# Operand tiles of the MLP's up weights at 24 offsets inside larger buffers

## The chip, the cores and the metric

The kernel runs on one core of a Trainium2 chip. The metric is device time in microseconds (us). Engines: TensorE (PE, its weight load PEld), VectorE (DVE), ScalarE (ACT), GpSimd (POOL) and SyncE (SP), whose queue issues the DMA transfers here.

## The reference

One layer with 1024 tokens of width 1024, in float32: an RMS norm, one input projection, two groups of heads in parallel (differential attention and a gated delta rule), an output projection added to the input, and then a squared-ReLU MLP of hidden width 4096. The change lies in the MLP's first half:

```python
h = rms_norm(x, norm2_w[l])
x = x + jnp.square(jax.nn.relu(h @ w_up[l])) @ w_down[l]
```

## The kernel before

Float32 products are made from a high and a low half: a tensor is cast to `fp32r` (the high half, on ScalarE), the cast is subtracted from the original (the low half, on VectorE), and TensorE multiplies high by high, low by high and high by low, three matmuls for one. `split` does the two steps.

The up stage multiplies `w_up` by the normed tokens. It saves products by Strassen's scheme (in Winograd's form): per group `g` of 512 hidden columns (8 groups) the weights come as four raw tiles a, b, c, d of 128 x 1024 elements, the tokens as four blocks and their differences (`hH`, `hL` and `T0h` to `T2l`), and seven products, numbered 1 to 7, take the place of eight. A product is 24 matmuls of 512 columns (2 column halves x 4 blocks x 3). "Product (0,6)" below is product 6 of group 0.

Products 3, 5, 6 and 7 need a sum or difference of raw tiles, made on VectorE (`combine`, L1443). The weights of a product then become an operand, a pair of tiles named `op`: the cast (L1447 in `rounded`, L1243 in `split`) and the subtraction (L1451 in `rest`, L1244 in `split`). The pool has five `op` buffers of 128 x 1024 elements, used in turn; they are TensorE's stationary operand, the tokens its moving one (`prod_up`, L1324 to L1326). After a product ScalarE or VectorE reads its PSUM bank (X, Y or Z) and forms the results `ua`, `b`, `c`, `ud`, `s`, which SP stores to DRAM for the down stage (`flush`, L1437). SP also loads the raw tiles (L1416), each when its buffer is free.

The first products of group 0 and 1 use operands made earlier, in the weight buffers of the stages before (`first_ops`: `wH0`, `wH1`, `wL0`): products (0,1), (0,2), (1,1), (1,2), in that order, into X0, Y, X1 and Z. X1's stationary operand in its first product lies in `wH1`. Then come (0,5), (0,6), (0,3), (0,7), (1,5), (0,4), (1,6), and so on. The operands of (0,5), (0,6), (0,3) and (0,7) are made by `rounded` and `rest`, in an order written out by hand.

A buffer may take memory that an earlier stage has given up; its first writer then waits for that tile's last reader. The five `op` buffers lie at the top of the memory that the weight buffers leave. In the built program the first `op` buffer begins at byte 208704 of a partition, where the raw buffers `wraw` were (208128 to 212287), and the last ends at 229184. `wH1` was at 199488 to 207807, `wL0` at 212288 to 220607. Below the `op` buffers lie `s`, `c`, `ud` and `b`.

Up to the marker `seam.close()` the order of TensorE, VectorE and ScalarE is the order of the code; behind it TensorE alone keeps the code's order, and a scheduler places VectorE's and ScalarE's instructions by its own model of their times.

The last stage multiplies the results by `w_down` (`down`, L1619 to L1621).

Of the kernel before, what the change touches and what calls it, by code (L numbers as in the profile page):

```python
# [10 lines left out]
F32R = mybir.dt.float32r  # L11
# [7 lines left out]
P = 128  # L19
# [98 lines left out]
def tile_hymba_layer(  # L118
# [491 lines left out]
    for h, hf, y, th in skew(dn_proj(1)):  # L610
# [6 lines left out]
        for c in range(4):  # L617
            i = cidx(h, 4 * hf + c)
# [9 lines left out]
        for c in range(4):  # L628
            i = cidx(h, 4 * hf + c)
# [49 lines left out]
    for h, hf, q2 in skew(dn_proj(0)):  # L679
# [6 lines left out]
        for c in range(4):  # L686
            i = cidx(h, 4 * hf + c)
# [3 lines left out]
        for c in range(4):  # L691
            i = cidx(h, 4 * hf + c)
# [548 lines left out]
    def split(dst, src):  # L1241

        S.copy(dst[0], src)  # L1243
        V.tensor_tensor(dst[1], src, dst[0].bitcast(F32), ALU.subtract)  # L1244
# [147 lines left out]
    op_ = octx.enter_context(tc.tile_pool(name="op", bufs=1, **right))  # L1392
# [16 lines left out]
    def load_w(g, names):  # L1409
        if g < NG:  # L1410
            u.setdefault(g, {})
            for n in names:
# [3 lines left out]
                nc.sync.dma_start(t, w_up_v[:, (k1, k2)[i % 2], c:c + 256])  # L1416
                w.setdefault(g, {})[n] = t

    def operand(src):
        o = [op_.tile([P, 4, 256], F32R, tag="op", name="op", bufs=5) for _ in range(2)]  # L1420
        split(o, src)
        return o

# [15 lines left out]
    early = {}  # L1439
# [3 lines left out]
        V.tensor_tensor(w[g][dst], w[g][l], w[g][r], op)  # L1443

    def rounded(g, i):
        early[g, i] = [op_.tile([P, 4, 256], F32R, tag="op", name="op", bufs=5) for _ in range(2)]
        S.copy(early[g, i][0], w[g][CH[i]])  # L1447

    def rest(g, i):
# [9 lines left out]
    held(2, [0, 1])  # L1459
    combine(0, 5)  # L1460
    rounded(0, 5)
    held(0, [2, 3])
    held(1, [2])
    rest(0, 5)
    held(1, [3])
    read_first()
    combine(0, 6)
    rounded(0, 6)
    combine(0, 3)
    held(2, [2, 3])  # L1470
# [4 lines left out]
    def product(g, i):  # L1475
# [10 lines left out]
        else:  # L1486
            bank = [x[:, p] for p in range(2)]
        o = early.pop((g, i), None) or (operand(w[g][CH[i]]) if g > 1 or i > 2 else None)
        for p in range(2) if o else ():
            for _ in prod_up(bank[p], o, p, H_OPS[i], i in (1, 2, 5) or (i == 4 and last), i in (2, 3, 4)):  # L1490
# [45 lines left out]
    def step(g, i):  # L1536
        puts.append([])
        product(g, i)
        flush(2)

    rounded(0, 3)
    step(0, 5)
    rest(0, 3)
# [154 lines left out]
```

## Time and profile before

| what | value |
|---|---|
| median of 3 runs | 1269.35 us (1268.46 to 1269.78) |
| profiled execution: span from first to last instruction | 1272.0 us; the page gives no other time of that execution |
| TensorE busy | 1238.8 us, 97% of the span |
| VectorE, ScalarE, GpSimd busy | 842.6, 602.7, 212.3 us |
| up stage, first and last matmul on `op` tiles | starts 673.61 us and 956.47 us |
| down stage | from 958.53 us to the end |

The rows below are of three kinds. A row of the timeline has the start in us, the duration in us, the engine, the line, the operation, its output and inputs, its shape and count, and in brackets the idle time of the engine before it with what ended it. A row of a tile or line has the durations in ns (least/median/most) and the first and last start. A row of a stretch has, for each engine, the busy us and the instructions, then the granted clock, the DMA engines' share and GB/s. Buffer numbers are left out of names: X is X0 or X1.

### The profile page before, as it was taken

What the parts mean: (1) busy time and instruction counts of PE and PEld (TensorE: products, weight loads), DVE (VectorE), ACT (ScalarE), POOL (GpSimd) and SP (SyncE); (2) the same over time, 40 slices, a digit from 0 to 9 for tenths busy, and PEclk for the clock granted to TensorE, in tenths of its full rate; (3) what the DMA queues carried; (4) which work ended last, traced back from release to release, by engine and by line L of the source; (5) the groups of instructions that cost most, each with busy time, mean ns of one, the idle gap of its engine ahead of it and who ended that gap; (6) DMA issues with size and microseconds to landing.
All of it is one profiled execution on the core that took longest, in us unless ns stands there. A gap on an engine that the chain in (4) does not pass through costs nothing.

```text
span 1272.0 us, 18929 instructions
## 1 busy us (share of the span) xinstructions
PE 1238.8 (97%) x6928; PEld 1066.1 (84%) x6928; DVE 842.6 (66%) x1406; ACT 602.7 (47%) x1176; POOL 212.3 (17%) x240
## 2 busy tenths in 40 slices
PE   8999999999999899999999999999999999999998
PEld 7977888898998898888878888888887788888886
DVE  5569798467727775776689656655667865677553
ACT  5354554334445565655467445445554333333331
POOL 1038222135543542122210000000000000000000
PEclk9999999999998999999999999999999999999999
DMA  7134554367674665333354545443368855422311
GB/s 251 50 108 110 152 163 126 82 189 236 214 212 143 191 191 168 100 107 92 130 172 160 204 149 182 160 154 116 132 211 323 325 198 199 165 100 100 125 41 66
DMA packets 164757, 200.29 MB, mean 157 GB/s; under 512 B 20224, under 2 KB 124984, under 8 KB 164664
## 3 DMA queue, kind: packets, MB, share of 16 engines
q1 hardware_dynamic: 164664, 199.08, 47.4%
q8 instruction: 55, 0.90, 0.3%
q14 instruction: 38, 0.31, 0.1%
HBM read 132.97 MB, written 66.06 MB: 156 GB/s over the span
## 4 chain that ended last, share of the span: by engine, by line
PE 86%; DVE 7%; DMA 3%; issue 2%; ACT 1%; POOL 1%; SPq 1%; DVEq 0%; POOLq 0%; ACTq 0%
PE X L1326 5%; PE X L1324 5%; PE X L1325 5%; PE X L1620 4%; PE X L1621 4%; PE X L1619 4%; PE ps_qk L909 3%; PE ps_qk L910 3%; PE ps_qk L911 3%; PE Y L1326 2%; PE Y L1324 2%; PE Y L1325 2%; PE ps_dn L202 2%; PE ps_o L1070 2%; PE ps_dn L204 2%; PE ps_dn L203 2%
## 5 line engine op out<-in xcount | busy, mean ns | idle before, releaser
L1243 ACT CAST hH<-ur 128x1024 fp32r<-128x1024 f32 x56 | 58.7, 1050 | 176.5 <-PE Z L1620 86.0
L1244 DVE TENSOR_TENSOR hL<-ur,hH 128x1024 fp32r<-128x1024 f32 x56 | 68.4, 1223 | 84.8 <-ACT hH L1243 84.7
L909 PE MATMUL ps_qk<-wH,hH 128*128 128x256 f32 x384 | 115.3, 300 | 0.0
L910 PE MATMUL ps_qk<-wL,hH 128*128 128x256 f32 x384 | 109.8, 286 | 0.0
L911 PE MATMUL ps_qk<-wH,hL 128*128 128x256 f32 x384 | 109.7, 286 | 0.0
L1244 DVE TENSOR_TENSOR op<-raw,op 128x1024 fp32r<-128x1024 f32 x48 | 58.7, 1223 | 74.1 <-PE X L1325 36.9
L1620 PE MATMUL X<-hL,hH 128*128 128x512 f32 x224 | 87.8, 392 | 2.1 <-DVE hL L1244 2.1
L1619 PE MATMUL X<-hH 128*128 128x512 f32 x224 | 87.5, 391 | 1.7 <-DVE b L1521 1.7
L1621 PE MATMUL X<-hH,hL 128*128 128x512 f32 x224 | 87.6, 391 | 0.0
L202 PE MATMUL ps_dn<-hH,wH 128*128 128x512 f32 x192 | 76.8, 400 | 1.7 <-ACT cp L525 1.7
L203 PE MATMUL ps_dn<-hL,wH 128*128 128x512 f32 x192 | 76.3, 397 | 0.0
L204 PE MATMUL ps_dn<-hH,wL 128*128 128x512 f32 x192 | 75.9, 396 | 0.0
L910 PEld LDWEIGHTS ps_qk<-wL,hH 128*128 128x128 f32 x384 | 74.6, 194 | 0.2
L909 PEld LDWEIGHTS ps_qk<-wH,hH 128*128 128x128 f32 x384 | 74.7, 195 | 0.0
L911 PEld LDWEIGHTS ps_qk<-wH,hL 128*128 128x128 f32 x384 | 74.4, 194 | 0.0
L1244 DVE TENSOR_TENSOR hL<-dw,hH 128x1024 fp32r<-128x1024 f32 x56 | 68.1, 1218 | 4.8 <-ACT hH L1243 4.8
L1243 ACT CAST op<-raw 128x1024 fp32r<-128x1024 f32 x48 | 50.4, 1051 | 35.7 <-PE Y L1326 19.9
L1243 ACT CAST hH<-dw 128x1024 fp32r<-128x1024 f32 x56 | 58.4, 1047 | 13.8 <-PE Z L1621 7.4
L197 POOL TENSOR_TENSOR wL<-wraw,wH 128x512 fp32r<-128x512 f32 x40 | 51.9, 1311 | 69.9 <-ACT wH L196 47.5
L529 DVE SCALAR_TENSOR_TENSOR cy<-cp,pv,cy 128x512 f32<-128x512 f32 x72 | 57.6, 804 | 7.9 <-ACT cy L527 7.2
L1031 ACT ACTIVATE pexp<-ps_sc,mx 128x128 f32<-128x128 f32 (+7 forms) x64 | 47.3, 741 | 25.9 <-DVE mx L1027 25.4
L1027 DVE TENSOR_REDUCE mx<-ps_sc 128x1 f32<-128x128 f32 (+7 forms) x64 | 47.6, 753 | 16.1 <-PE ps_sc L1025 15.5
(360 smaller groups left out, 3527.4 us busy)
## 6 DMA issues: line engine op xcount, KB each, us to landing
ur<-ud SPq DMA_DIRECT2D x28, 1024.0 KB, 4.9
raw<-in_w_up_dram SPq DMA_DIRECT2D x32, 512.0 KB, 3.9
dw<-in_w_down_dram SPq DMA_DIRECT2D x32, 512.0 KB, 6.5
wraw<-in_w_in_dram SPq DMA_DIRECT2D x48, 256.0 KB, 3.2
qk_d<-qa SPq DMA_DIRECT2D x32, 256.0 KB, 2.9
ud<-ua SPq DMA_DIRECT2D x16, 512.0 KB, 3.0
ud<-s SPq DMA_DIRECT2D x16, 512.0 KB, 2.6
pka<-park_d SPq DMA_DIRECT2D x32, 192.0 KB, 3.6
```

The lines of the kernel that those rows point to most:

```text
L202: T.matmul(ps, lh(k), rh(k), start=(k == 0), stop=False)
L203: T.matmul(ps, lh(k), rl(k), start=False, stop=False)
L204: T.matmul(ps, ll(k), rh(k), start=False, stop=(k == n - 1))
L909: T.matmul(ps[:, :256], hH[:, k, sl], wh[:, k, :], start=(k == 0), stop=False)
L910: T.matmul(ps[:, :256], hH[:, k, sl], wl[:, k, :], start=False, stop=False)
L911: T.matmul(ps[:, :256], hL[:, k, sl], wh[:, k, :], start=False, stop=(k == KB - 1))
L1243: S.copy(dst[0], src)
L1244: V.tensor_tensor(dst[1], src, dst[0].bitcast(F32), ALU.subtract)
L1324: T.matmul(ps, op[0][:, k, cs], h[0][:, k, :], start=start and k == 0, stop=False, skip_group_check=True)
L1619: T.matmul(bank[t], v[0][:, j, sl], v[2][:, j], start=s0, stop=False, skip_group_check=True)
L1620: T.matmul(bank[t], v[0][:, j, sl], v[3][:, j], start=False, stop=False, skip_group_check=True)
L1621: T.matmul(bank[t], v[1][:, j, sl], v[2][:, j], start=False, stop=s1, skip_group_check=True)
```

## The change

Each `op` tile becomes 128 x 1088 elements, and the 1024 elements in use begin at an offset that goes by turn: the first tile of pair n at entry n of a list of 24 offsets, the second at entry 7n + 3, both modulo 24. The offsets run from 0 to 60 elements of 4 bytes. Both places that make operands, `operand` and `rounded`, get their pairs from the new function.

```diff
+    SHIFTS = (0, 1, 2, 3, 4, 5, 6, 7, 8, 10, 12, 14, 16, 18, 20, 24, 28, 32, 36, 40, 44, 48, 52, 60)
+    made = [0]
+
+    def op_pair():
+        n, k = made[0], len(SHIFTS)
+        made[0] += 1
+        return [op_.tile([P, 1088], F32R, tag="op", name="op", bufs=5)[:, s:s + 1024].rearrange("p (k c) -> p k c", k=4)
+                for s in (SHIFTS[n % k], SHIFTS[(7 * n + 3) % k])]
+
     def operand(src):
-        o = [op_.tile([P, 4, 256], F32R, tag="op", name="op", bufs=5) for _ in range(2)]
+        o = op_pair()
         split(o, src)
         return o
...
     def rounded(g, i):
-        early[g, i] = [op_.tile([P, 4, 256], F32R, tag="op", name="op", bufs=5) for _ in range(2)]
+        early[g, i] = op_pair()
         S.copy(early[g, i][0], w[g][CH[i]])
```

No instruction is added or taken away. In the built program the `op` buffers now begin at 207424, 211776, 216128, 220480 and 224832; `s`, `c`, `ud` and `b` lie 1280 bytes lower, and 207424 lies inside what was `wH1`. The first cast into `op` (L1447 before, L1456 now) accordingly waits for the last matmul into X1 that reads `wH1`, where it had waited for the last matmul into Y that reads `wL0`; both also wait for the combined raw tile. TensorE's order is unchanged. Lines from L1419 on are 9 higher than before.

On VectorE some rows behind the operand of (0,7) change places. The engine's rows before, from the low half of operand (0,7) on; the next two operands are those of (1,5) and (0,4):

```order
L1451 TENSOR_TENSOR op<-raw,op 128x1024
L1244 TENSOR_TENSOR T2l<-kept,T2h 128x4x128 x2
L1443 TENSOR_TENSOR raw<-raw 128x1024
L1244 TENSOR_TENSOR T2l<-kept,T2h 128x4x128 x2
L1497 TENSOR_TENSOR ua_8488<-ua_8488,Z_8309 128x512
L1497 TENSOR_TENSOR ua_8488<-ua_8488,Z_8310 128x512
L1505 TENSOR_TENSOR c<-c,Y 128x1024
L1244 TENSOR_TENSOR op<-raw,op 128x1024 x2
L1510 TENSOR_TENSOR ud<-ud,X_7845 128x1024
L1443 TENSOR_TENSOR raw<-raw 128x1024
L1507 TENSOR_TENSOR s_8521<-ua_8383,c 128x1024
L1443 TENSOR_TENSOR raw<-raw 128x1024 x2
```

The same stretch of the change:

```order
L1460 TENSOR_TENSOR op<-raw,op 128x1024
L1452 TENSOR_TENSOR raw<-raw 128x1024
L1244 TENSOR_TENSOR T2l<-kept,T2h 128x4x128 x4
L1506 TENSOR_TENSOR ua_8488<-ua_8488,Z_8309 128x512
L1506 TENSOR_TENSOR ua_8488<-ua_8488,Z_8310 128x512
L1244 TENSOR_TENSOR op<-raw,op 128x1024
L1514 TENSOR_TENSOR c<-c,Y 128x1024
L1452 TENSOR_TENSOR raw<-raw 128x1024 x2
L1244 TENSOR_TENSOR op<-raw,op 128x1024
L1519 TENSOR_TENSOR ud<-ud,X_7845 128x1024
L1516 TENSOR_TENSOR s_8521<-ua_8383,c 128x1024
L1452 TENSOR_TENSOR raw<-raw 128x1024
```

The combination for (1,5) now stands ahead of the four rows of `T2l`, the operand of (1,5) ahead of `c<-c,Y`, and two combinations ahead of the operand of (0,4). On ScalarE one cast moves; before:

```order
L1370 ACTIVATE c<-c 128x1024
L1371 ACTIVATE c<-c 128x1024
L1370 ACTIVATE ud<-ud 128x1024
L1371 ACTIVATE ud<-ud 128x1024
L1243 CAST op<-raw 128x1024
L1501 COPY ud<-Y 128x1024
```

and of the change:

```order
L1370 ACTIVATE c<-c 128x1024
L1371 ACTIVATE c<-c 128x1024
L1243 CAST op<-raw 128x1024
L1370 ACTIVATE ud<-ud 128x1024
L1371 ACTIVATE ud<-ud 128x1024
L1510 COPY ud<-Y 128x1024
```

The cast of the operand of (1,6) goes ahead of the two steps on `ud`. On SP the first store of `s` goes ahead of the first store of `ud`, with two raw buffers exchanged.

## The prediction

> **What bounds the kernel now.** I read the page's first two lines, then the stretches of the up stage, then TensorE's rows in order of time, then what stands at the start of the stage on ScalarE and VectorE.
>
> ```profile
> span 1272.0 us, 18929 instructions
> PE 1238.8 (97%) x6928; PEld 1066.1 (84%) x6928; DVE 842.6 (66%) x1406; ACT 602.7 (47%) x1176; POOL 212.3 (17%) x240
> ...
> 850.00:900.00 50.00, 50.00 (x222) 41.42 (x221) 28.69 (x26) 25.35 (x25) 0.00 (x0) 1.00 0.41 149
> ```
>
> TensorE is busy for 97% of the span. The third row is a stretch inside the stage that the change touches: TensorE full, VectorE 57%, ScalarE 51%, granted clock 1.00.
>
> ```profile
> 679.29 0.39 PE L1325 MATMUL X<-T0l,op 128*128 128x512 f32 x1
> 679.58 0.50 PE L1326 MATMUL X<-T0h,op 128*128 128x512 f32 x1
> ...
> 956.47 0.39 PE L1326 MATMUL X<-T2h,op 128*128 128x512 f32 x1
> 958.53 0.50 PE L1619 MATMUL X<-hH 128*128 128x512 f32 x1 [1.68 <-DVE b L1521]
> ...
>   PEld X L1326: 0.3, 1
> ```
>
> From the row at 679.58 (the third matmul of product (0,6)) to the one at 956.47 (the last of the stage) stand 51 products of 24 matmuls less 3, or 1221 intervals: 276.89 / 1221 = 0.2268 us each, the spacing seen between any two neighbours. So no operand is late in all that time, and what is added there once is not made up later. The last row, from the waits on `op`, is the one wait of TensorE for an operand tile: L1326 at 679.58 waits for VectorE. It came 0.29 us after its neighbour instead of 0.23, so VectorE is about 0.06 us late at that place, and has no room there at all.
>
> **The chain behind that wait.** The rows of ScalarE, VectorE and TensorE at the seam:
>
> ```profile
> 666.73 1.05 ACT L1447 CAST op<-raw 128x1024 fp32r<-128x1024 f32 x1 [2.40 <-DVE raw L1443]
> 667.69 1.13 ACT L1270 CAST hH<-hn 128x512 fp32r<-128x512 f32 x2
> 673.45 1.06 ACT L1370 ACTIVATE ua<-ua 128x1024 f32<-128x1024 f32 x1 [3.72 <-DVE ua L1364]
> 676.45 1.14 ACT L1243 CAST T0h<-hn 128x512 fp32r<-128x512 f32 x2
> ...
> 668.34 0.69 DVE L1273 TENSOR_TENSOR hL<-hn,hH 128x512 fp32r<-128x512 f32 x1 [0.51 <-ACT hH L1270]
> 669.67 1.22 DVE L1451 TENSOR_TENSOR op<-raw,op 128x1024 fp32r<-128x1024 f32 x1
> 672.20 1.21 DVE L1364 TENSOR_TENSOR ua<-ua,Y 128x1024 f32<-128x1024 f32 x1
> 677.10 1.29 DVE L1244 TENSOR_TENSOR T0l<-hn,T0h 128x512 fp32r<-128x512 f32 x2 [1.28 <-ACT T0h L1243]
> 678.31 1.22 DVE L1451 TENSOR_TENSOR op<-raw,op 128x1024 fp32r<-128x1024 f32 x1
> ...
> 667.94 0.39 PE L1326 MATMUL X<-hH,wH 128*128 128x512 f32 x1
> 678.84 0.39 PE L1326 MATMUL Y<-hH,op 128*128 128x512 f32 x1
> 679.26 1.01 ACT L1501 COPY ud<-Y 128x1024 f32<-128x1024 f32 x1 [0.72 <-PE Y L1326]
> 674.08 0.39 PE L1326 MATMUL Y<-hH,op 128*128 128x512 f32 x1
> ```
>
> Read as a chain: the first cast of an operand (666.73) is followed by the casts into `hH` (667.69); VectorE's L1273 waits for the first of them (668.34) and runs without a gap to L1364 (672.20); ScalarE's L1370 waits for that (673.45) and runs on to the cast of `T0h` (676.45); VectorE waits for it (677.10), then makes the low half of operand (0,6) (678.31, ended 679.53), for which TensorE waits (679.58). Each link waits for the one before; none has slack.
>
> **The change, part by part.**
>
> *The larger first buffer.* The operand pool grows downwards by 5 x 256 bytes, and its first buffer now begins inside the old `wH1`. `wH1` is the stationary operand of the product into X1, whose last matmul is the row at 667.94, ended 668.33. The first cast now waits for it; before it waited for L1443 alone and began at 666.73. It begins at about 668.36, since the copy at 679.26 starts 0.03 us after the matmul that it waits for (678.84 + 0.39): 1.63 us later. Behind it in ScalarE's queue stand the casts into `hH`, so the chain above moves by 1.63 us as a whole, and operand (0,6) is ready at 679.53 + 1.63 = 681.16. Product (0,5), at 674.08, is covered: its low half ends at 669.67 + 1.63 + 1.22 = 672.52. Product (0,6) is not: its third matmul goes at 681.2 instead of 679.58, and TensorE stands for **1.6 us** more.
>
> *The rows that changed places on VectorE.*
>
> ```profile
> 688.99 1.22 DVE L1443 TENSOR_TENSOR raw<-raw 128x1024 f32<-128x1024 f32 x1
> 693.66 1.22 DVE L1244 TENSOR_TENSOR op<-raw,op 128x1024 fp32r<-128x1024 f32 x1
> 695.58 0.39 PE L1324 MATMUL Y<-hH,op 128*128 128x512 f32 x1
> 701.02 0.39 PE L1324 MATMUL X<-T2h,op 128*128 128x512 f32 x1
> 684.36 0.37 SPq L1416 DMA_DIRECT2D raw<-in_w_up_dram  x1
> 684.00:688.00 4.00, 4.00 (x19) 3.32 (x18) 4.00 (x7) 3.10 (x6) 0.00 (x0) 1.00 0.42 131
> ```
>
> `c<-c,Y`, which frees bank Y for product (1,5), now stands behind operand (1,5): it ends where that operand ended, 693.66 + 1.22 = 694.88, plus the shift 1.63, or 696.5; TensorE, also shifted, wants Y at 695.58 + 1.63 = 697.2. Cover 0.7 us. L1443 moves up by two half-size rows (about 1.2 us), to 689.4 after the shift, and reads a load that was issued at 684.36. Its 0.524 MB are the whole of the 131 GB/s x 4 us in the last row, so it had landed by about 688.2; issued 1.63 later it lands at 689.8. That costs 0.4 us of the 0.7 us cover: I take 0, and 0.5 us as the upper end if the load is slower. The two instances of L1443 that now stand ahead of operand (0,4) delay it and the update of `ud` behind it, which frees X for product (0,4): four rows of at most 1.22 us after 696.5 make 701.4, wanted at 701.02 + 1.63 = 702.65. Cover 1.2 us, cost 0. The rows that change places on ScalarE and SP feed only stores of results.
>
> *The offsets themselves.* Rows in which something reads or writes at an odd place, beside aligned ones:
>
> ```profile
> L525 ACT COPY cp<-ps_dn x24: 565/580/611, 78.6 to 240.7; 128x512 f32<-128x512 f32 x24
> L240 ACT CAST hH<-ps_tr x38: 564/587/620, 16.1 to 645.9; 128x512 fp32r<-128x512 f32 x38
> 135.82 0.75 DVE L529 SCALAR_TENSOR_TENSOR cy<-cp,pv,cy 128x512 f32<-128x512 f32 x1
> 136.60 0.75 DVE L529 SCALAR_TENSOR_TENSOR cy<-cp,pv,cy 128x512 f32<-128x512 f32 x1
> L1244 DVE TENSOR_TENSOR op<-raw,op 128x1024 fp32r<-128x1024 f32 x48 | 58.7, 1223 | 74.1 <-PE X L1325 36.9
> L1243 ACT CAST op<-raw 128x1024 fp32r<-128x1024 f32 x48 | 50.4, 1051 | 35.7 <-PE Y L1326 19.9
> L1324 PEld LDWEIGHTS Y<-hH,op x128: 186/188/188, 673.5 to 944.9; 128*128 128x128 f32 x128
> 508.57 1.78 PE ps_o L1070 x16
> ```
>
> L525 writes 3 elements into its tile and takes 580 ns, L240 writes aligned and takes 587: ScalarE's casts cost nothing. The two rows of L529 read the same tile from 1 and from 0 elements in, 0.75 us each: VectorE's reads cost nothing. VectorE's odd writes and TensorE's odd weight loads stand in no row. For the loads: sixteen matmuls of 128 columns take 1.78 us, 111 ns each, weight load included, so a load needs at most 111 ns of the 227 ns between two matmuls here and may double unseen. For the writes, the nearest row is ScalarE's odd write, 0; the other end is a doubled L1244, 1.22 us more, which L1451 meets twice in the chain above. I take 0 for both.
>
> [...]
>
> **The sum.** 1.6 + 0 + 0 = +1.6 us. The stop shifts all that follows: the down stage's loads start on TensorE's and VectorE's progress. The profiled span, 1272.0, becomes 1273.6; it lies 2.65 us above the median of the runs, 1269.35, and carried over as a difference the forecast is 1269.35 + 1.6 = **1271.0 us**.
>
> **Rivals.** Changes under 0.2%, about 2.5 us here, can hardly be told from none.
>
> ```profile
> 22.99 1.07 PE L235 MATMUL ps_tr<-ident,hn 128*128 128x128 f32 x8 [1.48 <-DVE hn L249]
> 79.20 0.50 PE L202 MATMUL ps_dn<-hH,wH 128*128 128x512 f32 x1 [1.67 <-ACT cp L525]
> 1004.67 0.80 PE L1620 MATMUL X<-hL,hH 128*128 128x512 f32 x1 [2.05 <-DVE hL L1244]
> 1004.67:1008.17 3.50, 3.50 (x8) 2.82 (x9) 3.50 (x6) 0.83 (x1) 0.00 (x0) 0.51 1.03 410
> 79.20:83.18 3.98, 3.98 (x10) 3.12 (x11) 1.25 (x5) 3.41 (x7) 1.45 (x5) 0.57 0.54 132
> ```
>
> 1. *The stop trips the clock* (slower, 0.22). After idle times of 1.67 and 2.05 us the granted clock was 0.57 and 0.51 for 4.0 and 3.5 us, and 8 matmuls took 3.50 us instead of 8 x 0.227 = 1.81: 1.7 us lost. After 1.48 us (22.99) and 1.68 us (958.53) it held. The new idle time is 681.20 - 679.68 = 1.5 us, on the mild side of both. If it trips: 1.6 + 1.7 = 3.3 us, 1272.7. [...]
> 2. *Offsets cost after all* (slower, 0.22). VectorE's odd writes, twice in the chain: from 0.5 us each it decides, 1.6 + 1.0 = 2.6, 1272.0; at the doubled 1.22, 1.6 + 2.4 = 4.0, 1273.4. Weight loads only beyond 227 - 111 = 116 ns more each; then every ns counts in 52 products of 24 matmuls, 1.2 us.
> 3. *The later stop is absorbed, and more* (faster, 0.06). At 1004.67 TensorE idles 2.05 us and loses 1.7 to the clock. If that wait hung on loads that do not move with the stop, TensorE would come 1.6 later, idle 0.4 and keep its clock: +1.6 - 1.6 - 1.7, 1267.7. It decides if the loads start on something earlier than the stop. Against it: they stand behind the stores of the up stage on one queue.
> 4. *The wait is no wait* (0.05). The cast's new condition is met early: 1269.35.
>
> **How the numbers follow.** My case has 0.45, with 1269.8 to 1271.7 as its own range (a shorter chain; the load's 0.5). With rival 4 that makes 0.50 within 0.2%, rivals 1 and 2 make 0.44 slower, rival 3 0.06 faster. The range 1268.8 to 1274.0 leaves out rival 3 and the far part of rival 2, some 0.15.
>
> **What would show it.** Right: L1456 on ScalarE starts at 668.4 behind X's last matmul; one wait of about 1.6 us of L1326 for `op` near 681.2; from there to the stage's end 0.227 us per matmul; casts, subtractions and weight loads on `op` at 1051, 1223 and 188 ns at every offset. Wrong: a granted clock near 0.5 at 681 (rival 1), a spread of L1244 or L1460 on `op` (rival 2), the idle time before the second down product gone (rival 3), the cast still at 666.7 (rival 4).

## The result, and the profile after

| | before | change |
|---|---|---|
| median of 3 runs | 1269.35 us | 1278.53 us (1278.09 to 1278.91) |
| ratio, 95% interval | 1 | 1.0065 (1.0047 to 1.0084), or +6.0 to +10.7 us |
| span of the profiled execution | 1272.0 us | 1276.4 us |
| up stage, from the last matmul on `wH` tiles to the last on `op` tiles | 283.09 us | 290.55 us |

The change made the kernel slower by 9.2 us; 1271.0 was forecast, 1268.8 to 1274.0 was the range. The two spans can't be compared directly: the last matmul on `wH` came at 673.38 us before and at 670.66 after, and in the runs below that leave all instructions and tokens ahead of it alone it lay anywhere from 669.82 to 675.13. So stages are compared with stages.

The top of the page of the change:

```profile
span 1276.4 us, 18928 instructions
PE 1240.5 (97%) x6928; PEld 1062.1 (83%) x6928; DVE 843.7 (66%) x1406; ACT 602.2 (47%) x1176; POOL 212.1 (17%) x240
```

It says nothing of the cause: TensorE is busy for 97% as before, with the same number of matmuls, and VectorE and ScalarE have the same work.

The stretch from 700 to 950 us lies inside the up stage, with TensorE full in both kernels. First before, then the change (busy us and instructions for PE, PEld, DVE, ACT, POOL; then the granted clock, the DMA share, GB/s):

```profile
700.00:950.00 250.00, 250.00 (x1105) 207.01 (x1104) 145.91 (x130) 123.40 (x123) 0.00 (x0) 1.00 0.46 164
```

```profile
700.00:950.00 250.00, 250.00 (x1082) 203.09 (x1081) 141.16 (x126) 121.77 (x122) 0.00 (x0) 1.00 0.44 159
```

TensorE is 100% busy at clock 1.00 in both, and still does 1082 matmuls where it did 1105. A matmul's row lasts 0.39 us, so the rows that touch 250 us are N = 250.39 / spacing, where spacing is the time from one matmul's start to the next: 226.6 ns before, 231.4 ns now (from the starts themselves 226.7 and 231.4). That is the main finding, and it can't be seen in any busy share, since rows of 0.39 us overlap at either spacing and TensorE looks busy all the same. The 52 products on `op` tiles are 1248 matmuls with 1247 intervals; 1247 x 4.7 ns = 5.9 us.

The trace of the change already ties this to the offsets. The list has 24 entries, so products 24 apart have the same two offsets. Their spacings, the mean of the last 12 intervals of each, agree within 0.42 ns, whichever tokens and PSUM bank they use, and lie between 226.7 ns (offsets 0 and 12 bytes) and 233.4 ns (16 and 28 bytes).

The casts, subtractions and weight loads of `op` in the change, by group (busy us and mean ns of one; for the load least/median/most ns):

```profile
L1244 DVE TENSOR_TENSOR op<-raw,op 128x1024 fp32r<-128x1024 f32 x48 | 58.7, 1223 | 78.2 <-PE X L1325 38.8 <-PE Y L1325 26.9 <-issue 7.8
L1243 ACT CAST op<-raw 128x1024 fp32r<-128x1024 f32 x48 | 50.3, 1048 | 37.5 <-PE Y L1326 20.7 <-PE X L1326 9.2 <-PE Z L1326 7.2
L1326 PEld LDWEIGHTS Y<-hH,op x128: 186/188/193, 672.8 to 949.9; 128*128 128x128 f32 x128
```

VectorE's odd writes take 1223 ns as before, ScalarE's 1048 (1051 before), a weight load 188. No single instruction that touches an odd address got longer; only the time from one matmul to the next did.

The seam, in the timeline of the change (start, duration, engine, line, operation, and in brackets the idle time and what ended it):

```profile
665.23 0.39 PE L1326 MATMUL X<-hH,wH 128*128 128x512 f32 x1
...
665.70 1.05 ACT L1456 CAST op<-raw 128x1024 fp32r<-128x1024 f32 x1 [4.08 <-PE X L1326]
...
670.66 0.39 PE L1326 MATMUL Z<-hH,wH 128*128 128x512 f32 x1
...
671.17 1.22 DVE L1364 TENSOR_TENSOR ua<-ua,Y 128x1024 f32<-128x1024 f32 x1
...
672.44 0.50 PE L1324 MATMUL Y<-hH,op 128*128 128x512 f32 x1 [1.39 <-DVE ua L1364]
...
678.54 0.51 PE L1326 MATMUL X<-T0h,op 128*128 128x512 f32 x1
...
961.21 0.40 PE L1326 MATMUL X<-T2h,op 128*128 128x512 f32 x1
```

The same place before:

```profile
672.20 1.21 DVE L1364 TENSOR_TENSOR ua<-ua,Y 128x1024 f32<-128x1024 f32 x1
...
673.38 0.39 PE L1326 MATMUL Z<-hH,wH 128*128 128x512 f32 x1
...
673.61 0.40 PE L1324 MATMUL Y<-hH,op 128*128 128x512 f32 x1
```

The first cast into `op` now waits for the last matmul of X1, as forecast, and TensorE stops once: 672.44 - 670.66 is 1.78 us instead of 0.23, a stop of 1.55 us. But it stops at the first matmul of product (0,5), for VectorE's L1364, and not at product (0,6). Together: 1.55 + 5.9 = 7.4 us, against 290.55 - 283.09 = 7.46 us in the stage.

Two more places of the change: TensorE's first matmuls after the stop, and the wait in the down stage with the 3.6 us behind it:

```profile
672.40:676.00 3.60, 3.56 (x16) 2.96 (x17) 2.34 (x2) 3.55 (x5) 0.00 (x0) 1.00 0.34 97
```

```profile
1009.06 0.50 PE L1629 MATMUL X<-hL,hH 128*128 128x512 f32 x1 [2.05 <-DVE hL L1244]
```

```profile
1009.90:1013.50 3.60, 3.60 (x11) 2.84 (x9) 3.60 (x6) 0.00 (x0) 0.00 (x0) 0.55 1.03 410
```

The stop at 672 left the granted clock at 1.00; the wait of 2.05 us in the down stage is there as before, with the clock at 0.55 behind it. So neither rival 1 nor rival 3 took place.

The same wait of 2.05 us stands in the trace of every kernel below, but the clock behind it is not always the same. With all offsets 0 (a kernel of the next section):

```profile
1003.18 0.50 PE L1624 MATMUL X<-hL,hH 128*128 128x512 f32 x1 [2.05 <-DVE hL L1244]
```

```profile
1003.18:1006.78 3.60, 3.60 (x16) 2.96 (x17) 3.60 (x6) 0.84 (x1) 0.00 (x0) 1.00 1.03 411
```

In six of the 14 traces the clock fell behind this wait for 3.4 us (before, change, 232 and 360 elements, the sweep, 164 bytes); in the other eight it stayed at 1.00, and the down stage took 311.8 us instead of 313.4 or 313.5. So the idle time alone doesn't decide it, though rival 1 took it to, and the time of one execution can differ by 1.6 us for this reason.

### The profile page after: what moved, and what is told of

The parts are those of the page before. It is cut to its first block, busy times and chain, and to the rows that moved or that the text cites. A ratio compares the mean times of both kernels' runs of the same rounds, so it can differ in the third digit from the quotient of the medians.

```text
span 1276.4 us, 18928 instructions
## 1 busy us (share of the span) xinstructions
PE 1240.5 (97%) x6928; PEld 1062.1 (83%) x6928; DVE 843.7 (66%) x1406; ACT 602.2 (47%) x1176; POOL 212.1 (17%) x240
## 4 chain that ended last, share of the span: by engine, by line
PE 79%; DVE 10%; DMA 5%; issue 2%; ACT 2%; POOL 1%; SPq 1%; DVEq 0%; POOLq 0%; ACTq 0%
PE X L1324 5%; PE X L1326 5%; PE X L1325 5%; PE X L1629 4%; PE X L1630 4%; PE X L1628 4%; PE Y L1324 2%; PE Y L1326 2%; PE Y L1325 2%; DMA wraw<-in_w_in_dram 2%; PE ps_o L1070 2%; PE ps_op L1157 2%; PE ps_op L1159 2%; PE ps_op L1158 2%; PE Z L1629 2%
## 5 line engine op out<-in xcount | busy, mean ns | idle before, releaser
L909 PE MATMUL ps_qk<-wH,hH 128*128 128x256 f32 x384 | 114.4, 298 | 0.0
L1244 DVE TENSOR_TENSOR op<-raw,op 128x1024 fp32r<-128x1024 f32 x48 | 58.7, 1223 | 78.2 <-PE X L1325 38.8
L911 PE MATMUL ps_qk<-wH,hL 128*128 128x256 f32 x384 | 108.8, 283 | 0.0
L202 PE MATMUL ps_dn<-hH,wH 128*128 128x512 f32 x192 | 76.3, 397 | 1.5 <-ACT cp L525 1.5
L204 PE MATMUL ps_dn<-hH,wL 128*128 128x512 f32 x192 | 75.2, 393 | 0.0
L909 PEld LDWEIGHTS ps_qk<-wH,hH 128*128 128x128 f32 x384 | 73.8, 192 | 0.0
L911 PEld LDWEIGHTS ps_qk<-wH,hL 128*128 128x128 f32 x384 | 73.4, 191 | 0.0
L1243 ACT CAST op<-raw 128x1024 fp32r<-128x1024 f32 x48 | 50.3, 1048 | 37.5 <-PE Y L1326 20.7
```

The source lines that it names most:

```text
L202: T.matmul(ps, lh(k), rh(k), start=(k == 0), stop=False)
L909: T.matmul(ps[:, :256], hH[:, k, sl], wh[:, k, :], start=(k == 0), stop=False)
L911: T.matmul(ps[:, :256], hL[:, k, sl], wh[:, k, :], start=False, stop=(k == KB - 1))
```

## The experiments

Below, "distance" is the byte address of the weight tile minus that of the moving tokens, modulo 256. Before the change all `op` tiles and all tokens (`hH`, `hL`, the T tiles) begin 64 bytes behind a multiple of 256, so the distance is 0. Times are against runs of the kernel before on the same chip; its medians there were 1270.74 us beside the first four kernels, 1271.44 beside the next four, 1271.16 beside the last four.

### One constant offset

In four kernels the wide tiles stay and all tiles get the same offset:

```diff
-                for s in (SHIFTS[n % k], SHIFTS[(7 * n + 3) % k])]
+                for s in (0, 0)]      # or (1, 1), (16, 16), (32, 32)
```

> The wide tiles of 1088 elements, but every offset 0: the pool begins inside the old wH1 as in the change, while each op tile begins 64 bytes behind a multiple of 256, as before the change. Theory A (the place of the weights in memory slows TensorE's stream, the pool's growth adds only a stop at product (0,5)): a stop of about 1.6 us near 671, then 226.7 ns from matmul to matmul; 1.6 us above the kernel before, 1271.0. Theory B (the wider pool itself, or what it does to the order of VectorE's rows, is the cause): 231 ns from matmul to matmul, 1278.5 as the change. Theory C (no theory needed for the wait): no stop, 1269.4.

> Wide tiles, every tile at offset 1 element (4 bytes), so every weight load begins 68 bytes behind a multiple of 256. If what counts is that the start isn't at a multiple of 16 or 64 bytes (A1): 231 ns or more from matmul to matmul, 6 us above the kernel with offset 0. If what counts is the distance to the 256-byte phase of the other operands (A2, any distance over some tens of bytes costs): 227 to 228.5 ns, 0 to 2 us above offset 0. If what counts is that the offset changes from tile to tile (A3): 226.7 ns, as offset 0.

> Wide tiles, every tile at offset 16 elements (64 bytes): aligned to 64 bytes, 128 bytes behind a multiple of 256. A1 (misalignment to 16 or 64 bytes): 226.7 ns, as offset 0, 1271. A2 (the phase within 256 bytes): in the change the products whose first operand lay at that phase were among the slowest, 233 to 234 ns; so 230 to 238 ns, 5 to 13 us above offset 0, 1276 to 1284. A3 (the change of offset from tile to tile): 226.7 ns.

> Wide tiles, every tile at offset 32 elements (128 bytes): 192 bytes behind a multiple of 256. A1 (misalignment): 226.7 ns, 1271. A2 (the phase within 256 bytes): 229 to 234 ns, 3 to 9 us above offset 0, 1274 to 1280. A3 (the change of offset from tile to tile): 226.7 ns.

| offset | distance | ratio, 95% interval | against before | up stage | mean spacing, 700 to 950 us, from the starts |
|---|---|---|---|---|---|
| 0 | 0 | 1.0021 (1.0007 to 1.0035) | +2.7 us (0.9 to 4.4) | 284.79 us | 226.7 ns |
| 1 element | 4 bytes | 1.0060 (1.0046 to 1.0073) | +7.6 us (5.8 to 9.3) | 291.72 us | 232.4 ns |
| 16 elements | 64 bytes | 1.0082 (1.0068 to 1.0097) | +10.4 us (8.6 to 12.3) | 292.88 us | 233.3 ns |
| 32 elements | 128 bytes | 1.0061 (1.0048 to 1.0073) | +7.8 us (6.1 to 9.3) | 291.72 us | 232.4 ns |

The stretch from 700 to 950 us of offset 0, then 1, 16 and 32:

```profile
700.00:950.00 250.00, 250.00 (x1105) 207.07 (x1104) 146.06 (x130) 125.24 (x124) 0.00 (x0) 1.00 0.46 164
```

```profile
700.00:950.00 250.00, 250.00 (x1078) 201.71 (x1077) 141.19 (x126) 121.68 (x121) 0.00 (x0) 1.00 0.44 158
```

```profile
700.00:950.00 250.00, 250.00 (x1073) 201.45 (x1072) 141.89 (x126) 122.35 (x121) 0.00 (x0) 1.00 0.44 157
```

```profile
700.00:950.00 250.00, 250.00 (x1077) 202.75 (x1076) 141.07 (x125) 121.28 (x120) 0.00 (x0) 1.00 0.44 158
```

With offset 0 the spacing is that of the kernel before, so theory B, the wide tiles themselves, falls; theory A's stop remains (672.32 - 670.54 - 0.23 = 1.55 us). A constant offset costs as much as a changing one (A3 falls), and an offset of 64 bytes costs more than one of 4 bytes (A1, misalignment to 16 or 64 bytes, falls). A2 is left, with one part of it wrong: I expected the price to grow with the distance, 0 to 2 us at 4 bytes, and 4 bytes cost nearly as much as 64. (The expectation for 64 bytes also misread the change: there the products whose first tile lay at 64 bytes took 231.2 ns, not 233 to 234.)

### The place of the tiles alone

The kernel before has an unused tile above the `op` pool (L1391). Its width moves all `op` tiles of 1024 elements down without making them wider:

```diff
-    octx.enter_context(tc.tile_pool(name="pad", bufs=1, **right)).tile([P, 40], F32, name="pad")
+    octx.enter_context(tc.tile_pool(name="pad", bufs=1, **right)).tile([P, 72], F32, name="pad")
```

> The kernel before with its op tiles of 1024 elements; only the unused tile of L1391 above the op pool is 72 elements wide instead of 40, so all op tiles lie 128 bytes lower, 192 bytes behind a multiple of 256. Every engine's order is that of the kernel before, and the pool doesn't reach wH1, so there is no stop. Theory P (the phase of the weight tile within 256 bytes, beside that of the tokens at 64, sets the spacing): 232.4 ns from matmul to matmul as with the constant offset of 128 bytes, 1246 x 5.6 ns = 7.0 us above the kernel before. Rival W (the wide tiles matter, by their stride of 4352 bytes or the changed order on VectorE): 226.7 ns and the time before.

Measured: 1.0068 (1.0056 to 1.0080), or +8.6 us (7.1 to 10.2); the same stretch:

```profile
700.00:950.00 250.00, 250.00 (x1078) 202.71 (x1077) 142.58 (x127) 121.90 (x121) 0.00 (x0) 1.00 0.44 158
```

232.4 ns from the starts, as with the wide tiles at 128 bytes; the up stage took 290.04 us instead of 283.09, +6.95, and TensorE had no stop at its start. No instruction, order or tile size is changed here, only addresses by 128 bytes: those of `op`, and with them those of `s`, `c`, `ud` and `b`, which lie below the pool. The offsets of 0 and of 32 elements part the two: there these four stay in one place, `op` alone moves by 128 bytes, and the spacing is 226.7 and 232.4 ns. So the place of the weights alone makes the loss. (The 7.0 us worked out for it lie just below the interval of the whole time, 7.1 to 10.2; what makes the rest is not known.)

With 232 and with 360 elements in the same line the tiles move by 768 and 1280 bytes, three and five times 256:

> The kernel before with the unused tile of L1391 at 232 elements instead of 40: the op tiles of 1024 elements lie 768 bytes lower, again 64 bytes behind a multiple of 256, and the first begins at 207936, just above the end of wH1 (207808). VectorE's, ScalarE's and SP's rows behind operand (0,7) change places as in the change. So it shows the reorder alone, and whether the effect repeats every 256 bytes. Theory P: 226.7 ns, no stop, the time before within 0.1%. Rival (the reorder or any move of the tiles costs): 1 us or more above it, or more than 227 ns between matmuls.

> The same at 360 elements: the op tiles 1280 bytes lower, again at 64, the first at 207424 inside the old wH1, as in the change; tiles of 1024 elements. Against the run with 232 elements only the overlap with wH1 is new. Theory: the first cast into op waits for the last matmul of X1, a stop of about 1.6 us of TensorE at the first matmul of product (0,5) for VectorE's L1364, 226.7 ns afterwards; 1.6 us above the run with 232 elements. Rival (the stop comes from the wide tiles): no stop, the time of that run.

| tile of L1391 | first `op` tile | distance | ratio, 95% interval | against before | up stage |
|---|---|---|---|---|---|
| 232 elements | 207936 | 0 | 1.0000 (0.9990 to 1.0011) | 0.0 us (-1.3 to +1.4) | 283.07 us |
| 360 elements | 207424, inside `wH1` | 0 | 1.0012 (0.9997 to 1.0027) | +1.5 us (-0.4 to +3.4) | 284.82 us |

The first cast with 232 elements, then the seam with 360:

```profile
668.46 1.06 ACT L1447 CAST op<-raw 128x1024 fp32r<-128x1024 f32 x1 [2.38 <-DVE raw L1443]
```

```profile
666.61 1.05 ACT L1447 CAST op<-raw 128x1024 fp32r<-128x1024 f32 x1 [3.87 <-PE X L1326]
...
671.58 0.39 PE L1326 MATMUL Z<-hH,wH 128*128 128x512 f32 x1
673.35 0.50 PE L1324 MATMUL Y<-hH,op 128*128 128x512 f32 x1 [1.38 <-DVE ua L1364]
```

The first run has all the exchanged rows of VectorE, ScalarE and SP that the change has, and costs nothing: the reorder is free, and a move of 768 bytes leaves the spacing as it was (1104 matmuls from 700 to 950 us, 1105 before), as one of 1280 bytes does in the second run (1104). The second adds only the overlap, and with it the cast waits for X and TensorE stops for 673.35 - 671.58 - 0.23 = 1.54 us. The interval of its time holds both 1.6 and 0; the trace settles it.

### Absolute place or distance

Two more kernels tell whether the place of the weights counts, or their distance to the tokens. `neghalf`, 128 bytes, is taken from ahead of `hH` and `hL` to behind them:

```diff
     hpool = ctx.enter_context(tc.tile_pool(name="hpool", bufs=1))
+    const2 = ctx.enter_context(tc.tile_pool(name="const2", bufs=1))
...
-    neghalf = const.tile([P, 32], F32, name="neghalf")
+    neghalf = const2.tile([P, 32], F32, name="neghalf")
```

> The kernel before with the constant neghalf placed behind hH and hL instead of ahead of them, so these two lie 128 bytes lower, 192 bytes behind a multiple of 256; op and the T tiles stay at 64. Theory P1 (what counts is the distance within 256 bytes between the weight tile and the moving tokens): products with hH and hL as tokens, 28 of 52 on op tiles, about 232 ns, those with T tiles 226.7 ns. P2 (the absolute place of the weight tile counts): 226.7 ns in all, time as before in the up stage. P3 (the absolute place of each operand counts): hH products slow, T products 226.7, as P1; the next run parts it from P1. The stages before use hH too and may change as well.

> Both edits: hH and hL 128 bytes lower and the op tiles 128 bytes lower, so these lie at 192 and the T tiles at 64. P1 (the distance counts): products with hH and hL 226.7 ns, products with T tiles 232 ns, the reverse of the run with the tokens alone moved. P2 (the weight's absolute place): 232 ns in all. P3 (the absolute place of each operand): 232 ns or more in all, most in the hH products.

Three first matmuls of neighbouring products, 24 matmuls each, with the tokens moved alone (lines are 1 higher here):

```profile
708.64 0.39 PE L1325 MATMUL X<-T0h,op 128*128 128x512 f32 x1
...
714.09 0.40 PE L1325 MATMUL X<-hH,op 128*128 128x512 f32 x1
...
719.68 0.40 PE L1325 MATMUL Y<-hH,op 128*128 128x512 f32 x1
```

The same three with tokens and `op` moved:

```profile
706.67 0.40 PE L1325 MATMUL X<-T0h,op 128*128 128x512 f32 x1
...
712.27 0.39 PE L1325 MATMUL X<-hH,op 128*128 128x512 f32 x1
...
717.73 0.39 PE L1325 MATMUL Y<-hH,op 128*128 128x512 f32 x1
```

With the tokens alone moved the product on T0 takes 5.45 / 24 = 227.1 ns a matmul, that on `hH` 5.59 / 24 = 232.9; with both moved it is 5.60 / 24 = 233.3 on T0 and 5.46 / 24 = 227.5 on `hH`. Over all products: T 227.1 and `hH` 233.1 in the first, T 233.1 and `hH` 227.0 in the second. The slow and the fast products change places, so it is the distance between the two operands that counts (P1); P2 and P3 fall. The times, 1278.03 and 1275.47 us, are one execution each and also hold what the stages before make of the moved `hH`. The stage of L202 to L204 has the same form, with its weights in `wH` and `wL`, which stay where they are: over its 576 matmuls the distance goes from 0 to 128 and the median spacing from 227 to 232 ns. The 1152 matmuls of L909 to L911 have 256 moving columns, and there `hH` and `hL` are the weights: with the distance of 128 the median stays at 119 to 120.

### All distances

> Wide tiles; pair n of operands has both tiles at offset 5n modulo 64 elements, 52 of the 64 places, so each product of 24 matmuls shows the spacing of one distance between weights and tokens. Theory P: a spacing that depends on the distance, from 226.7 ns at 0 up to 234 ns, mean 231 ns, and the same value for the tokens hH and T; the question is whether any distance gives less than 226.7 ns, which would make a kernel faster than both; I expect none. Rival (any distance but 0 costs the same): 232 to 233 ns everywhere. Time 1277 to 1280.

```diff
+        s = 5 * made[0] % 64
...
+                for _ in range(2)]
```

The first matmul of the product at distance 164 and that of the next product; then the same for distance 244:

```profile
792.80 0.40 PE L1324 MATMUL X<-hH,op 128*128 128x512 f32 x1
...
798.50 0.39 PE L1324 MATMUL Y<-hH,op 128*128 128x512 f32 x1
...
815.30 0.39 PE L1324 MATMUL Y<-hH,op 128*128 128x512 f32 x1
...
820.75 0.40 PE L1324 MATMUL X<-T2h,op 128*128 128x512 f32 x1
```

5.70 / 24 = 237.5 ns against 5.45 / 24 = 227.1 ns. From the starts in ns, the mean of the last 12 intervals within each product (when the spacing has settled), at 24 of the 52 distances:

```
bytes    4     8    12    20    24    28    32    44    60    64    84   100
ns   232.3 230.6 230.0 233.3 230.0 235.0 233.3 230.0 230.0 233.3 235.0 230.0
bytes  120   124   128   132   160   164   192   204   212   240   244   248
ns   226.7 233.3 232.6 226.7 233.3 238.9 228.9 236.3 236.7 228.3 226.7 233.3
```

26 of the 52 lie at 233.0 to 233.6; 120, 132 and 244 bytes are as good as 0; none is below 226.7. So none of the 52 places makes a kernel faster than the one before by this way; 12 more multiples of 4 were not tried. The mean from 700 to 950 us was 232.3 ns, and the time 1282.6 us, one execution: both above what was expected, 231 ns and 1277 to 1280.

Here both tiles of a pair have the same offset. In the change they differ, and the spacing can't be read off either one: the pair at 20 and 80 bytes took 230.0 ns, while 20 bytes for both took 233.3 and 80 for both 232.2; the pair at 28 and 16 took 226.8, while 28 for both took 235.0.

Two distances of this table were then held for the whole stage:

> Wide tiles, every tile at offset 30 elements (120 bytes). In the sweep the product at this distance kept 226.7 ns. If the distance of weights and tokens alone sets the spacing (P1), 226.7 ns from matmul to matmul in all products, though the offset is neither 0 nor a multiple of 16 bytes; about 1271 as with offset 0. If the sweep's value came from what went before it (rival H, history), 230 to 233 ns.

> Wide tiles, every tile at offset 41 elements (164 bytes), the slowest distance of the sweep: 238.9 ns there. P1: 238 to 239 ns in all products, (238.9 - 226.7) x 1245 = 15.2 us and the stop's 1.6 above the kernel before, 1286. H: 232 ns as at most distances, 1278.

The stretch from 700 to 950 us at 120 bytes, then at 164:

```profile
700.00:950.00 250.00, 250.00 (x1104) 207.02 (x1103) 146.22 (x130) 124.46 (x124) 0.00 (x0) 1.00 0.45 164
```

```profile
700.00:950.00 250.00, 250.00 (x1055) 199.16 (x1055) 141.76 (x126) 119.80 (x118) 0.00 (x0) 1.00 0.42 153
```

226.7 and 237.3 ns from the starts, and 1269.86 and 1289.66 us in one execution each. At 120 bytes the up stage took 284.75 us, as with offset 0 (284.79). An offset of 120 bytes, no multiple of 16, costs nothing; one of 164 bytes costs (237.3 - 226.7) x 1247 = 13.2 us and the stop, and the up stage took 297.82 us, 14.73 more than before. So the value goes with the distance and not with what went before it (H falls). The 238.9 of the table was a little high: the intervals repeat in fives there, and 12 of them hold the longest more than its share. Fifteen intervals in ns from one matmul's start to the next, in the run at 164 bytes and, below, in the run at 4 bytes:

```
229 234 257 236 230 229 235 256 237 230 229 234 257 237 230
230 238 227 235 231 234 231 231 238 227 235 231 234 231 231
```

The pattern, of five and of seven, runs on across products, banks and tiles.

## Why the prediction was wrong

*The larger first buffer, +1.6.* Right in mechanism and size: the cast waited for X (665.70, idle 4.08), and the stop was 1.55 us in the change and 1.54 us with the overlap alone. Its place was wrong. "Product (0,5) is covered: its low half ends at 672.52" looked at the operand and not at bank Y, which L1364 frees; L1364 is a link of the same chain and had no slack either (ended 673.41, used from 673.61), so the size came out the same, which was luck: the wait that sets it was another than the one that was followed.

*The rows that changed places, 0.* Right: 0.0 us (-1.3 to +1.4) with 232 elements.

*The offsets themselves, 0.* This is the step that failed. "I take 0 for both" was true of VectorE's writes (1223 ns), and of the weight load taken by itself (188 ns); ScalarE's casts cost nothing either (1048 ns). But the sum needed the spacing of matmuls, and that rose by 4.7 ns, 5.9 us in all. The bound I used, that a load needs at most 111 ns of 227 and so "may double unseen", with a cost "only beyond 227 - 111 = 116 ns more each", would do for a load that only has to be ready in time. It leaves out that the matmuls themselves may come slower while each load is as long as before: the load of the next weights goes on beside the present matmul (188 of 227 ns), and the distance of the two operands in memory sets the spacing (226.7 ns at 0 and 232.4 at 128 bytes, with the load at 188 in both). The rows with 512 moving columns that I used all came from products with the distance 0, so they could not show it; the row that gave 111 ns is of 128 columns. The kernel gave a hint that I passed over: the unused tile of L1391 sets the `op` tiles to the same phase as the tokens, and 72 elements in the place of 40 cost 8.6 us (7.1 to 10.2).

*The sum.* 1.6 + 0 + 0 should have been 1.55 + 0 + 5.9 = 7.4, or 1276.8; measured +9.2 (6.0 to 10.7).

*The rivals.* Rival 2, offsets that cost after all, named the right part of the change with the wrong ways: neither VectorE's writes nor a load beyond 116 ns more. Its upper end, 1273.4, lay near the end of the range, 1274.0, since I gave the spacing no bound above zero where no row showed one. Rivals 1, 3 and 4 did not take place (clock 1.00 at 672; the 2.05 us at 1009 remain; the cast waits). Rival 1 rested on idle times that don't decide by themselves: the clock fell or held behind the same 2.05 us.

## What to carry to other kernels

A stretch in which TensorE is 100% busy at full clock can still be slow (1105 matmuls in 250 us before, 1055 at 164 bytes, both at clock 1.00): count its matmuls per stretch, or take the distance of two starts, before believing the busy share. Where weights are loaded beside running matmuls of 512 columns as here, their address modulo 256 against that of the moving operand is part of the design (128 bytes cost 5.7 ns a matmul); a tile that looks like mere padding may hold it in place (L1391 at 72 elements cost 8.6 us). And a price that no row shows is not zero because the nearest instruction has room: here each ns of spacing counted 1247 times.

## What the runs showed of the hardware

- With a weight tile of 128 columns and 512 moving columns of fp32r the spacing of matmuls depended on the distance of the two addresses modulo 256: 226.7 ns at 0, 120, 132 and 244 bytes, 230 to 234 at most others, 237.3 at 164 (both tiles of an operand at one distance). At a move of 768 or 1280 bytes the spacing was that of 0 (1104 matmuls in 250 us, 1105 before). The rows of the weight loads stayed at 186 to 193 ns, median 187 or 188, in the kernel before, the change, the four constant offsets and the runs with 232 and 360 elements.
- With 256 moving columns a distance of 128 cost nothing: 119 to 120 ns, and 120 at 0.
- It isn't alignment: 120 bytes cost nothing, 64 and 128 bytes cost 6.6 and 5.7 ns a matmul.
- After the stop the kernel with the wide tiles at offset 0 did not start at 226.7 ns: its first intervals in product (0,5) were 340, 240, 235, 234, 236, 224, 231, 235, 229, 232, 231 and then 227, 226, 227. There the spacing settled within some ten matmuls; the repeating patterns seen at 164 and at 4 bytes, of five intervals and of seven, differ with the distance. At one distance, 128, both a pattern of 232.4 ns and one of 233.3 ns were seen, the latter with tokens and `op` both moved, for T tiles at the same addresses; what parts the two was not shown.
- The weights' address alone makes a difference: between offsets of 0 and 32 elements only it changes, and they are 5.7 ns a matmul apart (226.7 and 232.4).
- Why the distance counts, and why four distances are free, was not shown by any run. That it is the load beside the matmul, and not another pair of accesses, is argued from the reversal with moved tokens, not shown. The sweep adds that it isn't the writing of operands: while the product at 120 bytes ran at 226.7 ns (709.28 to 714.72), VectorE and ScalarE wrote operands at 140 and 160 bytes, whose own products then took 233.3.
